# A decay table, modulation rows and one value half at other places in a two-layer backbone kernel

## The chip, the cores and the metric

The kernel runs on one core of a Trainium2 chip, in one launch. The metric is the device time of an execution in microseconds (us), as a median of several runs. TensorE (PE) multiplies matrices, VectorE (DVE) and ScalarE (ACT) work elementwise on tiles of 128 partitions, GpSimd (POOL) and SyncE (SP) here do little but issue transfers. Products land in PSUM, which has eight banks of 128 x 512 float32.

## The reference, cut to what matters

Latent tokens x (512 x 1024) and context tokens (256 x 1024) pass through two layers. Each layer normalises its input and modulates it with a shift, a scale and a gate computed from a conditioning vector:

```python
silu_c = jax.nn.silu(c)
for i in range(DEPTH):                       # DEPTH = 2
    shift_x, scale_x, gate_x = jnp.split(silu_c @ ada_w[i] + ada_b[i], 3, axis=-1)
    hx = rmsnorm(x, norm_g[i]) * (1 + scale_x[:, None]) + shift_x[:, None]
    # layer 0: retention over latent and context tokens; layer 1: chunked gMLP
    x = x + gate_x[:, None] * out_x
return rmsnorm(x, final_g)

def retention_mixer(hx, hc, w_in, decay_logit, w_out, need_ctx):
    log_g = jax.nn.log_sigmoid(decay_logit)
    qc, kc, vc, zc = retention_project(hc, w_in)     # 4 heads: q, k 256 wide, v, z 512 wide
    qx, kx, vx, zx = retention_project(hx, w_in)
    qx, kx = axial_rope(qx, row, col), axial_rope(kx, row, col)
    # scores q k^T times powers of the head's decay, in both directions, then times v
    out_x = retention_output(ox, zx, w_out)          # rmsnorm, times silu(z), times w_out
```

The output is the latent stream. Layer 0's context output is not needed for it.

## The kernel before, in words

**Numbers.** Products take float32 operands cut into a high and a low part (`split`, L132: ACT writes the high part with a CAST, DVE subtracts it to get the low part), and `mm3` (L126) does three matmuls for one. In the profile such a pair is `hl`: the CAST `hl<-raw` on ACT, then `hl<-raw,hl` on DVE.

**Projections of layer 0.** The input projection is worked off in pieces called kq, v and z of a head. Each piece is one 2x2 block product done by the seven products of a Strassen-like scheme, in the order `SINGLE` = B11, T1, T2, B21, T3, B22, T4. Each product is 24 matmuls of 128 x 256 (twelve more for the context tokens of a v piece, 24 for those of B11 and B21 of a kq piece). `Product.run` gives their banks: B11, T2, T3 and T4 share bank x; T1 and B22 share z; B21 has y. After B11, T1 and T2 ACT copies the bank away (`snap<-pst`, called snap); after B21, B22 and T3 DVE adds the bank onto such a copy (`snap<-snap,pst`, called plus). So T4 may write bank x only after the plus of T3 has read it. z and y are taken from a ring of two banks with the tag `tm`, and whatever else asks for a `tm` bank stands in the same ring.

**The loop that is changed (L1142).** It runs over nine pieces; I call them n = 0 to 8: kq1, v1, z1, kq2, v2, z2, z3, kq3, v3, the digit being the head. `i` counts the seven products within one. After a product, the text hangs other work there:

- `step()` is one step of `background` (L987): the modulation rows of the next layer, four pieces. One of the pieces 0 to 2 has twelve steps: one load, eight that multiply a row of weights by one conditioning number and add it up on DVE (`ada_a<-bg,cpad,ada_a`; a load of the next row stands ahead of each of the first seven), an empty one, then two for the columns. The first column step (`columns`, L968) takes a `tm` bank and does four matmuls `pst<-ada_a,ones`, and ACT copies the bank (`cole<-pst`). The second takes another `tm` bank for two transposes `pst<-ident,cole`, and DVE copies out 128 x 8. `row_tags` names the buffers that rows are loaded to, `bg_raw` deals them out in turn.
- `aside(dec0)` is one of three steps of `decay(0)` (L1039): a 512 KB table is loaded, ACT takes two exponentials of 128 x 512 (`bg<-bg,lg`), DVE combines them into `dt`. Head 0's attention needs `dt`.
- `aside(qk0)` and `aside(v0)` load head 0's q, k, v and z back from DRAM and cut them (`halves`, L1063: `v<-v` first on ACT, then on DVE).
- `between_modes` (L361) puts a `pst<-ones` matmul where the operands change from one kind to another.
- `popped` finishes a product of kq: rope on DVE (`rope_a`, `rope_b`) and a transfer to DRAM by POOL.

PE keeps the order of the text. On ACT and DVE a scheduler of the tile layer orders by its own estimates; an instruction written within `aside` may not stand ahead of the one before it in the text (`Queue`, L54, which is why nearly every row of the profile says L54).

After the loop comes `attend` (L1172) for head 0, whose third score product needs the bank that the first `pf<-pst,dt` of DVE has read (two `tm` banks again).

Of the kernel before, what the change touches and what calls it, by code (L numbers as in the profile page):

```python
# [67 lines left out]
def hybrid_kernel(ctx, tc, xT_d, cT_d, cv_d, sv_d, rows_d, ada0_d, adag_d, w_d, rope_d, dec_d, ws_d, id_d, out_d):  # L68
# [464 lines left out]
    g0 = sv[:, 32:48].rearrange("p (k r) -> p k r", r=2)  # L533
# [174 lines left out]
    def project(q):  # L708
        if q[0] == "kq":
            return Product(features, kq_done(q[1]), hc)  # L710
        if q[0] in ("v", "z"):
            return Product(tokens, wide_done(*q), ctx=(CA, vc_d[q[1]]) if q[0] == "v" else None)
        return Product(tokens, vz_done(q[1], q[2]), hc)
# [234 lines left out]
    row_tags = ["g0", "s3"]  # L948
# [76 lines left out]
    def aside(work):  # L1025

        act.pinned = dve.pinned = True
        r = next(work, None)
        act.pinned = dve.pinned = False
        return r  # L1030

    def step():
        return aside(bg)
# [67 lines left out]
    def load_v(h):  # L1101
        v = []
        for tag, src in zip(("oA11", "oS1", "oS2"), (*v_d[h], vc_d[h])):
            v.append(st([P, 2, 2, 512], tag, F32R, name="v"))
            load(f32(v[-1][:, 1]), src)
            yield
        z = st([P, NT, 512], "oA12", name="z")
        for t in range(2):
            load(z[:, 2 * t:2 * t + 2, :], z_d[h][t])
        yield  # L1110
        for x in v:
            halves(x)
            yield
        vv[h] = v, z
        yield

    def popped():
        if later:
            later.pop(0)()

    def drained(gen):
        for _ in gen:
            pass
# [15 lines left out]
    pieces = []  # L1139
    qk0 = load_qk(0)  # L1140
    v0 = load_v(0)
    for n, q in enumerate(QUADS[3:]):  # L1142
        pr = project(q)
        if n in (2, 6):
            row_tags[:] = ("g0", "s3", "g2") if n == 2 else ("s3", "g2")
        if n in (1, 4, 8):
            inside_t.append(between_modes)
        if n in (0, 3, 7):
            inside.append(between_modes)
        for i, name in enumerate(SINGLE):  # L1150
            pr.run(name, Q.get())
            if i in (1, 5) if n == 0 else i % 2:
                popped()
            if (n, i) in ((0, 3), (0, 5), (1, 0), (1, 2)):
                aside(ctx_sum)
            if 2 not in pieces and i in {0: (2, 4, 6), 1: (1, 3, 5, 6), 2: (1, 5), 5: (1, 5), 6: (1, 5)}.get(n, range(7)):
                pieces.append(step())
            if n == 6 and i % 2 == 0:
                aside(dec0)
            if n == 8:  # L1160
                aside(qk0)
                if i > 2:
                    aside(qk0)
            if n == 8:
                aside(v0)
    drained(dec0)
    drained(qk0)
    drained(v0)
# [585 lines left out]
```

## Time and profile before

| what | us |
|---|---|
| median of three runs | 870.85 (870.5 to 871.86) |
| the profiled execution's own time | 869.74 |
| its span in the profile | 868.0 |
| PE busy | 856.9 (99%) |
| DVE busy | 699.5 (81%) |
| ACT busy | 463.6 (53%) |
| POOL busy | 78.4 (9%) |

The span is the time from the first to the last recorded instruction; the execution's own time is 1.74 us longer. The mean granted PE clock is 0.998 of full speed. A row of a timeline reads: start, duration, engine, line, operation, out<-in, shapes, how many in a run, and in brackets the idle time of that engine just before, with what ended it. `snap<-snap,pst` on DVE is a plus, `snap<-pst` on ACT is a snap.

### The profile page before, as it was taken

The numbers are of one execution on the slowest core, as the hardware profiler recorded it, in microseconds if no ns is written. First come the engines' busy times: TensorE is split into PE (matmuls) and PEld (weight loads), VectorE is DVE, ScalarE is ACT, GpSimd is POOL, SyncE is SP. The second block draws the span as 40 slices with busy tenths as digits, with TensorE's granted clock in tenths as the row PEclk, the third lists the DMA queues.
The fourth block names the chain that finished last, engine by engine and source line by source line (L and its number), as shares of the span: only waits on it lengthen the run. The fifth ranks groups of instructions, "written<-read, shape, count | busy, mean of one in ns | idle before, by whom it ended". The sixth has DMA issues, their size and how long they took to land.

```text
span 868.0 us, 17070 instructions
## 1 busy us (share of the span) xinstructions
PE 856.9 (99%) x6870; PEld 819.6 (94%) x6870; DVE 699.5 (81%) x1007; ACT 463.6 (53%) x726; POOL 78.4 (9%) x119
## 2 busy tenths in 40 slices
PE   8999999999999999999999999999999999999997
PEld 7899999999999898999989899999999899899986
DVE  4799899869867985878676669998888478678895
ACT  5466644444368345727363549754667456255434
POOL 0001211211211010000000002021000000000110
PEclk9999999999999999999999999999999999999999
DMA  9945867877867898757164622666556256146522
GB/s 359 405 128 150 252 188 265 259 209 210 282 182 240 270 322 293 256 165 242 64 227 138 213 55 110 211 167 222 168 146 194 49 147 204 39 147 195 120 44 104
DMA packets 77551, 165.88 MB, mean 191 GB/s; under 512 B 8096, under 2 KB 33184, under 8 KB 77472
## 3 DMA queue, kind: packets, MB, share of 16 engines
q1 hardware_dynamic: 65856, 128.40, 44.1%
q0 software_dynamic: 11184, 36.18, 16.2%
q8 instruction: 54, 0.88, 0.4%
q10 hardware_dynamic: 432, 0.20, 0.1%
q14 instruction: 25, 0.20, 0.1%
HBM read 128.58 MB, written 24.12 MB: 176 GB/s over the span
## 4 chain that ended last, share of the span: by engine, by line
PE 74%; issue 12%; DVE 5%; DMA 5%; POOL 2%; ACT 1%; POOLq 0%; DVEq 0%; SPq 0%; ACTq 0%
PE pst L54 74%; DMA ada_w<-in_ada_dram 2%; DVE hl L54 2%; DMA bg<-in_adag_dram 1%; DVE ada_a L54 1%; DMA cq<-in_cT_dram 1%; POOL raw L186 1%; DVE rope_a L54 1%; DMA z<-snap 1%; DVE raw L54 1%; POOL z L142 0%; DMA cv<-in_cv_dram 0%; POOL v L142 0%; DVE o L54 0%; DVE cs L54 0%
## 5 line engine op out<-in xcount | busy, mean ns | idle before, releaser
L54 DVE TENSOR_TENSOR hl<-raw,hl 128x1024 fp32r<-128x1024 f32 (+2 forms) x197 | 235.4, 1199 | 70.5 <-ACT hl L54 70.1
L54 ACT CAST hl<-raw 128x1024 fp32r<-128x1024 f32 (+2 forms) x197 | 202.1, 1031 | 141.9 <-PE pst L54 59.3
L54 PE MATMUL pst<-hl,oS 128*128 128x256 f32 x1152 | 134.6, 276 | 0.0
L54 PEld LDWEIGHTS pst<-hl,oS 128*128 128x128 f32 x1152 | 132.3, 188 | 0.4 <-ACT ctx L54 0.4
L54 PE MATMUL pst<-oS,hl 128*128 128x256 f32 x1104 | 132.3, 277 | 0.0
L54 PEld LDWEIGHTS pst<-oS,hl 128*128 128x128 f32 x1104 | 128.1, 188 | 0.8 <-issue 0.8
L54 PE MATMUL pst<-oA,hl 128*128 128x256 f32 x936 | 117.0, 280 | 1.6 <-DVE snap L54 1.5
L54 PEld LDWEIGHTS pst<-oA,hl 128*128 128x128 f32 x936 | 110.7, 188 | 3.8 <-DVE snap L54 1.7
L54 PE MATMUL pst<-hl,oA 128*128 128x256 f32 x768 | 92.4, 277 | 0.0
L54 PE MATMUL pst<-og,hl 128*128 128x256 f32 x768 | 91.1, 278 | 0.0
L54 PEld LDWEIGHTS pst<-hl,oA 128*128 128x128 f32 x768 | 89.3, 188 | 0.4 <-ACT hl L54 0.4
L54 PEld LDWEIGHTS pst<-og,hl 128*128 128x128 f32 x768 | 89.2, 188 | 0.3
L54 DVE TENSOR_TENSOR raw<-raw 128x1024 f32<-128x1024 f32 x69 | 84.1, 1220 | 0.7
L54 ACT ACTIVATE snap<-pst 128x512 f32<-128x512 f32 x75 | 44.6, 595 | 67.2 <-PE pst L54 67.2
L54 PE MATMUL pst<-v,ph 128*128 128x512 f32 x192 | 59.8, 393 | 0.0
L54 PE MATMUL pst<-hl,ya 128*128 128x512 f32 (+1 forms) x246 | 59.1, 386 | 0.0
L186 POOL DMA_DIRECT2D raw<-raw x23 | 20.5, 891 | 388.3 <-ACT hl_e L54 173.3
L54 PEld LDWEIGHTS pst<-hl,ya 128*128 128x128 f32 x246 | 45.3, 188 | 9.4
L54 DVE TENSOR_TENSOR snap<-snap,pst 128x512 f32<-128x512 f32 x69 | 47.0, 681 | 5.8 <-PE pst L54 5.7
L54 ACT CAST ph<-pf 128x512 fp32r<-128x512 f32 x24 | 14.8, 618 | 57.3 <-DVE pf L54 57.3
L54 PEld LDWEIGHTS pst<-v,ph 128*128 128x128 f32 x192 | 36.1, 188 | 7.0
L54 DVE SCALAR_TENSOR_TENSOR acc<-pst,gate,acc 128x256 f32<-128x256 f32 x64 | 29.3, 479 | 12.8 <-PE pst L54 12.7
(207 smaller groups left out, 1105.2 us busy)
## 6 DMA issues: line engine op xcount, KB each, us to landing
raw<-in_w_dram SPq DMA_DIRECT2D x224, 256.0 KB, 3.9
bg<-in_adag_dram SPq DMA_DIRECT2D x32, 512.0 KB, 5.0
raw<-raw POOLq DMA_DIRECT2D x23, 512.0 KB, 4.7
ada_w<-in_ada_dram SPq DMA_DIRECT2D x16, 512.0 KB, 8.7
raw<-in_w_dram SPq DMA_DIRECT2D x16, 512.0 KB, 4.5
bg<-in_dec_dram SPq DMA_DIRECT2D x12, 512.0 KB, 5.4
v<-snap POOLq DMA_DIRECT2D x16, 256.0 KB, 4.1
z<-snap POOLq DMA_DIRECT2D x16, 256.0 KB, 3.9
```

The lines of the kernel that those rows point to most:

```text
L54: made = op(*args, **kw)
L186: nc.gpsimd.dma_start(self.raws[q, "12"], self.raws[q, "22"], accum_op=ALU.add)
```

## The change

Three things in the loop over n, and no arithmetic is changed:

- the three steps of head 0's decay table stand after products 1, 3 and 5 of n = 3 (q and k of head 2) where they stood after products 0, 2 and 4 of n = 6 (z of head 3);
- the steps of the modulation rows are dealt out anew: one more at n = 2, four for seven at n = 3, and three for two at n = 5 and n = 6. By the end of n = 6 both kernels have done 27, so n = 7 and 8 are as before. The buffers for rows go with it: `g0` is left out from n = 2 to n = 3 while the decay table uses it, and again from n = 7;
- after product 5 of n = 8 (v of head 3) a second step of `load_v(0)` follows the first.

```diff
     for n, q in enumerate(QUADS[3:]):
         pr = project(q)
-        if n in (2, 6):
-            row_tags[:] = ("g0", "s3", "g2") if n == 2 else ("s3", "g2")
+        if n in (2, 4, 7):
+            row_tags[:] = ("g0", "s3", "g2") if n == 4 else ("s3", "g2")
...
-            if 2 not in pieces and i in {0: (2, 4, 6), 1: (1, 3, 5, 6), 2: (1, 5), 5: (1, 5), 6: (1, 5)}.get(n, range(7)):
+            if 2 not in pieces and i in {0: (2, 4, 6), 1: (1, 3, 5, 6), 2: (1, 3, 5), 3: (0, 2, 4, 6), 5: (1, 3, 5), 6: (1, 3, 5)}.get(n, range(7)):
                 pieces.append(step())
-            if n == 6 and i % 2 == 0:
+            if n == 3 and i % 2:
                 aside(dec0)
...
             if n == 8:
                 aside(v0)
+                if i == 5:
+                    aside(v0)
```

How instructions move is shown at three places.

ACT in z of head 3 (n = 6), a piece of the difference (`bg<-bg,lg` are the exponentials, `snap<-snap` the silu of a finished block, `ACT_TABLE_LOAD` stands where ACT changes from one function to the other):

```order
-L54 ACTIVATE snap<-pst 128x512
-L54 ACT_TABLE_LOAD
-L54 ACTIVATE bg<-bg,lg 128x512 x2
-L54 ACTIVATE snap<-pst 128x512
-L54 CAST hl<-raw 128x1024 x2
-L54 ACTIVATE snap<-pst 128x512
-L54 ACTIVATE bg<-bg,lg 128x512 x2
-L54 CAST hl<-raw 128x1024 x2
-L54 ACT_TABLE_LOAD
-L54 ACTIVATE snap<-snap 128x512 x2
-L54 ACT_TABLE_LOAD
-L54 ACTIVATE bg<-bg,lg 128x512 x2
```

The six exponentials and all four changes of function leave this piece. Two changes are left in all: one ahead of the exponentials in kq of head 2, one ahead of the first silu in z of head 2.

PE in z of head 2 (n = 5), before, from the first product's `hl_2989` on (`oA11` is B11, `oS1` T1, `oS2` T2, `oA12` B21, `oS3` T3):

```order
L54 MATMUL pst_3086<-ada_a_2623,ones_126 32x256 x4
L54 MATMUL pst_3096<-hl_2989,oA11_328 128x256 x24
L54 MATMUL pst_3126<-hl_3041,oS1_861 128x256 x24
L54 MATMUL pst_3153<-ident_130,cole_3091 128x128 x2
L54 MATMUL pst_3156<-ones_126 128x128
L54 MATMUL pst_3096<-hl_3093,oS2_1012 128x256 x24
L54 MATMUL pst_3200<-hl_3123,oA12_570 128x256 x24
L54 MATMUL pst_3096<-hl_3161,oS3_1239 128x256 x24
```

and now:

```order
L54 MATMUL pst_3107<-hl_3003,oA11_328 128x256 x24
L54 MATMUL pst_3137<-hl_3058,oS1_861 128x256 x24
L54 MATMUL pst_3107<-hl_3104,oS2_1012 128x256 x24
L54 MATMUL pst_3203<-hl_3134,oA12_570 128x256 x24
L54 MATMUL pst_3231<-ada_a_2672,ones_126 32x256 x4
L54 MATMUL pst_3107<-hl_3164,oS3_1239 128x256 x24
L54 MATMUL pst_3137<-hl_3196,oS4_1173 128x256 x24
L54 MATMUL pst_3305<-ident_130,cole_3236 128x128 x2
```

The column step of the second row piece has moved from ahead of B11 to behind B21. Its `pst_3231` has the bank of `pst_3203`, since the other bank of the `tm` ring holds `pst_3137`, which B22 still adds to; it waits for the plus that reads `pst_3203`.

DVE at the end of v of head 3 (n = 8), before:

```order
L54 TENSOR_TENSOR v<-v 128x1024
L54 TENSOR_TENSOR snap<-snap,pst 128x512
L54 TENSOR_TENSOR ctx<-ctx,pst 128x256
L54 TENSOR_TENSOR v<-v 128x1024
L54 SCALAR_TENSOR_TENSOR pf<-pst,dt 128x512
```

and what the difference says there:

```order
 L54 TENSOR_TENSOR v<-v 128x1024
 L54 TENSOR_TENSOR snap<-snap,pst 128x512
+L54 TENSOR_TENSOR v<-v 128x1024
 L54 TENSOR_TENSOR ctx<-ctx,pst 128x256
 L54 TENSOR_TENSOR qk<-qk 128x512 x2
```

The last `v<-v` (the low part of head 0's context v) stands one product earlier, behind the plus of T3, and no longer right ahead of the first `pf`. Its CAST on ACT moves in the same way, ahead of T4's snap.

## The prediction, made before the result was known

> **What bounds the kernel now.** The profile's first part names the engine: PE is busy 856.9 of 868.0 us. So I looked for the holes in PE, first in its waits by what ended them (behind the start-up, one for a DVE `snap` and one for a DVE `pf`), then with windows between the two. Columns of a window: length, then busy time of PE, PEld, DVE, ACT, POOL (with counts), the granted clock, the DMA share, GB/s.
>
> ```profile
> 105.00:293.00 188.00, 187.97 (x1657) 186.70 (x1656) 162.83 (x201) 93.44 (x126) 31.52 (x47) 1.00 0.74 233
> 296.00:331.00 35.00, 35.00 (x310) 34.46 (x310) 27.13 (x41) 14.55 (x22) 5.46 (x9) 1.00 0.88 280
> ```
>
> From 105 to 331 us PE stands still in two places only, near 294 and near 331. The clock is 1.00 throughout. What the change can win lies in these two holes; what it can lose are new ones. A full PE does 48 matmuls in 200.72 - 195.28 = 5.44 us (first two rows below), 0.1133 each and 2.72 per product of 24.
>
> *The hole near 294* is in kq of head 3, between B22 and T4:
>
> ```profile
> 195.28 5.60 PE L54 MATMUL pst<-oS,hl 128*128 128x256 f32 x48
> 200.72 2.88 PE L54 MATMUL pst<-oA,hl 128*128 128x256 f32 x24
> ...
> 285.52 2.88 PE L54 MATMUL pst<-hc,hl 128*128 128x256 f32 x24
> 288.24 5.60 PE L54 MATMUL pst<-oS,hl 128*128 128x256 f32 x48
> 288.30 0.68 DVE L54 TENSOR_TENSOR snap<-snap,pst 128x512 f32<-128x512 f32 x1
> 294.61 0.68 DVE L54 TENSOR_TENSOR snap<-snap,pst 128x512 f32<-128x512 f32 x1
> 295.35 1.87 PE L54 MATMUL pst<-oA,hl 128*128 128x256 f32 x14 [1.50 <-DVE snap L54]
> 298.19 0.88 PE L54 MATMUL pst<-hl,oA 128*128 128x256 f32 x6
> ```
>
> T4 could start at 288.24 + 5.44 = 293.68; it starts at 295.35, and the next product at 298.19 instead of 296.40. The hole costs 1.79 us. T4 waits for the plus of T3 (294.61 + 0.68 = 295.29, and 0.06 more). DVE is late as a whole: it does B21's plus at 288.30, though PE left B21's latent part at 285.52, 0.20 before DVE could read (192.56 and 192.76 in kq of head 2, below). From plus to plus it is busy without a break, 295.29 - 288.30 = 6.99 us. Why it is late stands one piece earlier, in z of head 3:
>
> ```profile
> 256.08 1.28 ACT L54 ACT_TABLE_LOAD   x1
> 257.38 1.34 ACT L54 ACTIVATE bg<-bg,lg 128x512 f32<-128x512 f32 x2
> 261.47 1.33 ACT L54 ACTIVATE bg<-bg,lg 128x512 f32<-128x512 f32 x2
> 264.75 1.28 ACT L54 ACT_TABLE_LOAD   x1
> 269.45 1.28 ACT L54 ACT_TABLE_LOAD   x1 [1.45 <-DMA bg<-in_dec_dram]
> 270.75 1.34 ACT L54 ACTIVATE bg<-bg,lg 128x512 f32<-128x512 f32 x2
> 272.11 1.28 ACT L54 ACT_TABLE_LOAD   x1
> 273.94 1.03 ACT L54 CAST hl<-raw 128x1024 fp32r<-128x1024 f32 x1
> 272.12 0.69 DVE L54 TENSOR_TENSOR dt<-bg 128x512 f32<-128x512 f32 x1 [1.17 <-ACT bg L54]
> 275.00 1.23 DVE L54 TENSOR_TENSOR hl<-raw,hl 128x1024 fp32r<-128x1024 f32 x1 [2.19 <-ACT hl L54]
> ```
>
> ACT waits for the last table, changes its function and comes to kq3's first CAST at 273.94 only; DVE stands still for 1.17 and 2.19 us and never makes it up (19.53 us busy of the 20 from 276, in the windows below).
>
> *The hole near 331* is the third score product of head 0:
>
> ```profile
> 324.00 0.68 DVE L54 TENSOR_TENSOR snap<-snap,pst 128x512 f32<-128x512 f32 x1
> 328.31 2.99 PE L54 MATMUL pst<-qk 128*128 128x256 f32 x24
> 328.77 1.05 ACT L54 CAST v<-v 128x1024 fp32r<-128x1024 f32 x1
> 329.86 1.23 DVE L54 TENSOR_TENSOR v<-v 128x1024 fp32r<-128x1024 f32 x1 [4.84 <-ACT v L54]
> 331.00 0.68 DVE L54 SCALAR_TENSOR_TENSOR pf<-pst,dt 128x512 f32<-128x512 f32 x1
> 331.74 1.68 PE L54 MATMUL pst<-qk 128*128 128x256 f32 x12 [0.44 <-DVE pf L54]
> ```
>
> It could start at 328.31 + 2.72 = 331.03 and starts 0.71 later, because `pf` stands behind a `v<-v` whose CAST came last on ACT. With a slow second matmul, as in the other hole, I count 0.75.
>
> **The change part by part.** *Decay table out of z3.* ACT loses 1.34 + 1.33 + 1.34 + 4 x 1.28 = 9.13 us there, and DVE the `dt` work (0.69 for each full part, 0.76 for the divided one in a row below). B21's plus in kq3 must come 288.30 - 285.72 = 2.58 earlier to be on time; the last `dt` and the two standstills alone are 0.69 + 1.17 + 2.19 = 4.05. Then DVE's 6.99 end at 292.7 against 293.68: the hole goes, with 1.0 to spare. Steps at n = 7 are the same as before, so nothing is added in that stretch. -1.79; bounds -1.79 and, should half of the lateness stay, -0.9.
>
> *Decay table into kq2.* The windows say where DVE has room:
>
> ```profile
> 182.00:201.00 19.00, 18.96 (x169) 18.24 (x168) 11.51 (x16) 6.98 (x9) 2.27 (x3) 1.00 0.47 152
> 220.00:240.00 20.00, 20.00 (x180) 19.46 (x179) 17.03 (x24) 8.08 (x11) 5.86 (x9) 1.00 0.81 259
> 276.00:296.00 20.00, 18.50 (x163) 18.30 (x162) 19.53 (x21) 8.68 (x11) 2.44 (x4) 1.00 0.72 247
> ...
> 192.56 2.88 PE L54 MATMUL pst<-hc,hl 128*128 128x256 f32 x24
> 192.76 0.69 DVE L54 TENSOR_TENSOR snap<-snap,pst 128x512 f32<-128x512 f32 x1 [0.68 <-PE pst L54]
> 194.82 0.76 DVE L54 TENSOR_TENSOR rope_a<-rope_a,rope_b 128x256 f32<-128x256 f32 x2
> 198.97 0.68 DVE L54 TENSOR_TENSOR snap<-snap,pst 128x512 f32<-128x512 f32 x1
> 262.84 0.76 DVE L54 TENSOR_TENSOR dt<-bg 128x384 f32<-128x384 f32 x2 [0.30 <-ACT bg L54]
> ```
>
> In kq2 (182 to 201) DVE is idle for 7.5 us and ACT for 12. The first `dt` fits ahead of B21's plus. Between it and T3's plus stand now, in addition, one low half of `hl` (1.14 from row to row, as from 329.86 to 331.00; formerly ahead of B21's plus) and `dt` of 0.76. Laid end to end from 192.76: plus 0.60, low half 1.14, rope 2.1 (its last row ended at 195.58, 2.2 behind the plus), `dt` 0.7, low half 1.14, sum of two weights 1.14, plus 0.68, which ends near 200.3. T4 is due at 200.72: 0.4 to spare instead of 1.07 (198.97 + 0.68 = 199.65). If DVE absorbs nothing of the 1.90 added, the plus ends at 201.55 and T4 is 0.89 late. I take 0.10, since a missing 0.4 would need a late CAST.
>
> The Trainium skill ("ScalarE: Activation LUTs", What ACT_TABLE_LOAD costs) gives a change of function 1.28 us for the load and 1.38 more for a drain. The load is 1.28 in these rows too, but the next function starts 1.30 after the load's start both times (257.38, 270.75), so no drain shows. By the page the casts behind kq2's new change would be 1.38 later, and its T4 some 0.6 late: an estimate that ends at the second rival below.
>
> *Steps of the modulation rows.* The second piece's column step now follows B21 in z2 and needs the bank of B21. PE must wait until DVE has read it: 0.20 from PE's last result to DVE (192.56 to 192.76), 0.68 for the plus, 0.06 back to PE (295.29 to 295.35), together 0.94. Before, the same four matmuls stood ahead of B11 with no wait:
>
> ```profile
> 232.36 0.64 PE L54 MATMUL pst<-ada_a,ones 128*32 128x256 f32 x8
> 232.93 3.00 PE L54 MATMUL pst<-hl,oA 128*128 128x256 f32 x24
> 242.36 1.04 ACT L54 CAST hl<-raw 128x1024 fp32r<-128x1024 f32 x1
> 243.43 1.23 DVE L54 TENSOR_TENSOR hl<-raw,hl 128x1024 fp32r<-128x1024 f32 x1 [1.95 <-ACT hl L54]
> ```
>
> Nothing in the sequence lets PE go past it, so the whole round trip is lost. DVE is just free to take it. Without the matmuls of the column steps ahead of it PE comes to B21 at 232.36 + 3 x 2.72 = 240.52, 1.15 sooner than before; T4's CAST and low half (242.36 and 243.43 before) depend on ACT's copy of T2's bank and come sooner with it, at 241.21 and 242.28, and DVE is free at 243.44. PE leaves B21 at 243.24, readable at 243.44. I take 0.90, as the switch to another operand costs 0.12 in any place (232.36 to 232.93 is 0.57 for four matmuls). Bounds: 0 if the bank is read in time, 2.08 if that low half is first in the queue. Its followers lie later in z2 with 2 us to spare, so the delay is paid once.
>
> Two of the second piece's rows of `ada_a` (about 1.2 each from row to row) go on DVE from kq2 to the end of v2, where 2.97 us are idle (220 to 240). They stand ahead of T2's low half in z2, and so does now the low half of B21:
>
> ```profile
> 202.09 1.27 DVE L54 SCALAR_TENSOR_TENSOR ada_a<-bg,cpad,ada_a 128x1024 f32<-128x1024 f32 x1
> 232.81 2.45 DVE L54 TENSOR_TENSOR hl<-raw,hl 128x1024 fp32r<-128x1024 f32 x2 [1.17 <-ACT hl L54]
> ```
>
> T2's low half was done at 234.04 and comes to 234.04 + 1.14 + 2.4 - 1.17 = 236.4, with T2 due at 232.36 + 5.44 = 237.80; without the 1.17 of idle time as cover it comes at 237.57, still in time. So nothing. On SP the tables and rows are issued at other places of its queue, each where a buffer is free; no load of weights stands behind a new wait there.
>
> *v half one product sooner.* The last low half stands one product sooner, and what follows it on DVE moves by at most 1.14: B22's plus (324.00) then ends at 325.8, and PE next needs its bank at 328.31. Its load is issued where it was; should it land late, DVE waits for it ahead of T4's score banks, which is the bound of no gain. `pf` can start at 328.31 + 1.36 + 0.20 = 329.87, ends at 330.55, and the third score starts on time. -0.75; bounds -0.75 and 0.
>
> **Sum.** -1.79 - 0.75 + 0.90 + 0.10 = -1.54. The profiled execution's own time of 869.74 (span 868.0 and 1.74 around it) goes to 868.2; the median stands 1.11 above that execution, so **869.3**.
>
> **The rivals.** *No wait at the column step* (12%): DVE's plus is done before PE gets there, or PE finds another bank. For it: the column step of before shows no wait (232.36). Against it: that one found both banks free, and behind B21 nothing stands in between. Then -1.79 - 0.75 + 0.10 = -2.44, 868.4.
>
> *The hole moves to kq2* (20%): the added 1.90 us is not absorbed and T4 waits 0.89 there, or a part of the hole in kq3 stays: -1.54 - 0.10 + 0.89 = -0.75, 870.1. For it: only 0.4 us of room by my layout. Against it: DVE's 7.5 us of idle time in kq2. The drain of the Trainium skill leads here too.
>
> *DVE is full in both kq pieces* (8%, slower): kq3's hole isn't ACT's doing but DVE's, with 19.53 of 20 us busy; then it stays, and kq2, given the table, gets one of its own. It decides if B21's plus in kq3 still comes after 285.72 + 1.0 = 286.7. Then 0 - 0.75 + 0.90 + 0.89 = +1.04, 871.9. Against it: the standstills of 1.17 and 2.19 just ahead.
>
> *The moves change nothing that PE waits for* (4%): the holes stay, the column step finds its bank: 870.85.
>
> **How the numbers follow.** The forecast has 56%, with its own range 868.8 to 870.0 (0.5 for the column step and for kq2). A difference below 0.2%, 1.74 us, can't be told from none here; the border is at 869.11. The forecast lies just inside: a third of its chance falls beyond, 0.20; with the first rival and a few hundredths of the second I say faster 0.35, slower 0.08 (the rival that says so), and the rest, 0.57, no change. The range that holds 8 in 10 goes from 868.0, below the first rival, to 870.9, beyond the second.
>
> **What would show it.** Right: no wait for `snap` in kq3, with ACT's `hl` CASTs ahead of it near 269; no wait for `pf` near 331; a new wait of PE on DVE `snap` in z2, ahead of four `pst<-ada_a,ones`, with about 0.7 idle; B21's plus in kq3 0.2 after PE. Wrong: a hole ahead of T4 in kq2 over 0.3; a hole in kq3 left; a column step longer than 1.5; holes at some place that I haven't named, such as T2 of z2 waiting for `hl`.

## The result, and the profile after

The changed kernel takes 869.97 us (median of 20 runs, 868.54 to 871.71), the kernel before 871.85 in 20 runs beside it (870.5 to 873.23). The ratio is 0.9979, with a 95% interval from 0.9973 to 0.9986: 1.8 us less, between 1.2 and 2.4. The forecast was 1.5 less.

The profiled execution of the changed kernel took 870.49 us with a span of 868.7, which is longer than the profiled 869.74 and 868.0 of before. The profiled execution of before was faster than any of its 20 timed runs (the lowest is 870.50), that of the changed kernel slower than its median. So the spans alone would mislead; what counts is where PE stands still. The waits of PE after (us in total, times, longest):

```profile
PE pst L54 <- DMA ident<-in_id_dram: 1.9, 1, 1.9
PE pst L54 <- DVE eps L54: 1.1, 1, 1.1
PE pst L54 <- DVE snap L54: 0.8, 1, 0.8
PE pst L54 <- DVE pf L54: 0.2, 1, 0.2
```

The first two belong to the start-up. The one wait for a `snap` is a new one, in z of head 2; the one for `pf` is another than before, in head 1's scores. Laid out as in the prediction, windows after:

```profile
105.00:241.00 136.00, 135.97 (x1198) 135.24 (x1197) 122.48 (x159) 65.16 (x91) 22.78 (x35) 1.00 0.78 242
241.00:246.00 5.00, 4.22 (x40) 3.61 (x39) 3.12 (x4) 3.24 (x4) 0.00 (x0) 1.00 0.81 259
246.00:331.00 85.00, 85.00 (x751) 84.46 (x750) 67.52 (x83) 39.46 (x55) 14.80 (x22) 1.00 0.78 243
```

From 105 to 331 us there is one hole where there were two, at 244 to 245, and PE is full from 246 to 331.

A ledger over the whole span can be made from the trace, since both kernels start the same number of recorded matmuls (6870) in nearly the same order: the time from the start of matmul number a to that of number b, before and after.

```
stretch (matmul numbers)             before    after   difference
0 to 298     start-up                 34.53    35.48     +0.95
298 to 2030  up to v2                196.23   196.21     -0.02   (T4 of kq2 lies here)
2030 to 2145 z2 up to T3              12.91    13.75     +0.84   column step
2145 to 2560 up to B22 of kq3         47.14    47.15     +0.01
2560 to 2600 around T4 of kq3          6.32     4.53     -1.79
2600 to 2880 up to head 0's scores    31.76    31.72     -0.04
2880 to 2910 head 0's scores           5.17     4.44     -0.73
2910 to 3240 head 0's attention       44.83    45.01     +0.18
3240 to 3310 head 1's scores          11.43    12.06     +0.63
3310 to 4450                         152.46   152.53     +0.07
4450 to 4640 layer 1                  21.64    22.30     +0.66
4640 to the last matmul              296.26   296.26      0.00
```

The stretch from the start-up's end to matmul 2910, in which all the terms of the forecast lie, is 1.73 us shorter. Start-up (PE waits 1.9 for `ident<-in_id_dram` there, before 1.2) and three later entries, of 0.18, 0.63 and 0.66, add what makes this one execution longer; the later ones are taken up below.

The places themselves, in the timeline after. Kq of head 3:

```profile
269.25 1.05 ACT L54 CAST hl<-raw 128x1024 fp32r<-128x1024 f32 x1 [2.23 <-DVE raw L54]
287.29 2.88 PE L54 MATMUL pst<-hc,hl 128*128 128x256 f32 x24
287.49 0.69 DVE L54 TENSOR_TENSOR snap<-snap,pst 128x512 f32<-128x512 f32 x1
290.01 5.60 PE L54 MATMUL pst<-oS,hl 128*128 128x256 f32 x48
293.81 0.68 DVE L54 TENSOR_TENSOR snap<-snap,pst 128x512 f32<-128x512 f32 x1
295.45 2.88 PE L54 MATMUL pst<-oA,hl 128*128 128x256 f32 x24
```

ACT comes to kq3's first CAST at 269.25, where it came to it at 273.94 before, and now after a wait of 2.23 for DVE's `raw`. B21's plus begins at the first possible moment, 0.20 behind PE (before: 2.78 behind). T3's plus ends at 294.49, 0.96 ahead of T4, which follows B22 without a break (290.01 + 5.44 = 295.45).

Z of head 2, the column step:

```profile
241.35 2.88 PE L54 MATMUL pst<-hl,oA 128*128 128x256 f32 x24
243.12 1.23 DVE L54 TENSOR_TENSOR hl<-raw,hl 128x1024 fp32r<-128x1024 f32 x1 [1.49 <-ACT hl L54]
244.28 0.69 DVE L54 TENSOR_TENSOR snap<-snap,pst 128x512 f32<-128x512 f32 x1
245.02 0.64 PE L54 MATMUL pst<-ada_a,ones 128*32 128x256 f32 x8 [0.78 <-DVE snap L54]
```

B21 is through at 241.35 + 2.72 = 244.07. The plus starts at 244.28, 0.21 behind it and in the moment in which DVE has laid down a low half, and the four small matmuls start at 245.02, 0.95 late.

Kq of head 2 on ACT, DVE and PE, and head 0's first scores:

```profile
188.09 1.28 ACT L54 ACT_TABLE_LOAD   x1
189.38 1.33 ACT L54 ACTIVATE bg<-bg,lg 128x512 f32<-128x512 f32 x2
200.55 0.68 DVE L54 TENSOR_TENSOR snap<-snap,pst 128x512 f32<-128x512 f32 x1
201.65 2.88 PE L54 MATMUL pst<-oA,hl 128*128 128x256 f32 x24
...
324.71 0.68 DVE L54 TENSOR_TENSOR snap<-snap,pst 128x512 f32<-128x512 f32 x1
328.25 4.40 PE L54 MATMUL pst<-qk 128*128 128x256 f32 x36
329.86 0.69 DVE L54 SCALAR_TENSOR_TENSOR pf<-pst,dt 128x512 f32<-128x512 f32 x1 [4.13 <-PE pst L54]
```

T3's plus in kq2 ends at 201.23, 0.42 ahead of T4. The three score products run on as 36 matmuls; `pf` now waits for PE and not for a `v<-v`.

### The profile page after: what moved, and what is told of

The parts are those of the page before. It is cut to its first block, busy times and chain, and to the rows that moved or that the text cites. A ratio compares the mean times of both kernels' runs of the same rounds, so it can differ in the third digit from the quotient of the medians.

```text
span 868.7 us, 17062 instructions
## 1 busy us (share of the span) xinstructions
PE 858.7 (99%) x6870; PEld 822.4 (95%) x6870; DVE 698.8 (80%) x1007; ACT 461.4 (53%) x724; POOL 78.1 (9%) x119
## 4 chain that ended last, share of the span: by engine, by line
PE 94%; DMA 2%; DVE 1%; ACT 1%; issue 1%; ACTq 0%; DVEq 0%
PE pst L54 94%; DMA bg<-in_dec_dram 1%; DMA ident<-in_id_dram 1%; ACT junk L54 0%; DMA bg<-in_adag_dram 0%; DVE o L54 0%; ACT bg L54 0%; DVE acc L54 0%; DVE v L54 0%; DVE ada_a L54 0%; ACT L54 0%; DVE hl L54 0%; ACT hl L54 0%; ACT fss L54 0%; DVE dt L54 0%
```

## The experiments

Two questions stood open. Did the hole in kq3 go because ACT was freed in z3, or because the new wait in z2 gave DVE 0.8 us? And is the new wait the bank's, so that it can be had for nothing? A third came with the ledger: whether head 1 takes a part back. All ratios are against the kernel before, run on the same chip beside the others.

**The column step one product later.** The changed kernel with

```diff
-5: (1, 3, 5), 6: (1, 3, 5)}
+5: (1, 4, 5), 6: (1, 3, 5)}
```

> The changed kernel with one step moved: the column step of the second row piece stands behind T3 of z2 in place of behind B21. My theory: its bank was read one product earlier, so the new wait of about 0.8 us in z2 goes, and nothing else changes: no hole ahead of T4 in kq3, none near 331. That is about 2.6 us less than before, a ratio near 0.9970 (the changed kernel's is 0.9979). Rival 'the wait pays for the hole': kq3's hole is closed only because the wait in z2 gave DVE 0.8 us; then a hole of about 0.8 comes back ahead of T4 in kq3, and the ratio stays near 0.9979. Rival 'given back in head 1': PE comes earlier to the attention of head 1 and waits there for a table that comes by its own clock, so the ratio stays near 0.9979 with a hole near 380 that is 0.8 longer.

868.93 us, ratio 0.9964 (0.9952 to 0.9976). Z of head 2 in its timeline:

```profile
241.14 2.88 PE L54 MATMUL pst<-hl,oA 128*128 128x256 f32 x24
243.86 2.88 PE L54 MATMUL pst<-hl,oS 128*128 128x256 f32 x24
246.67 0.64 PE L54 MATMUL pst<-ada_a,ones 128*32 128x256 f32 x8
247.24 3.00 PE L54 MATMUL pst<-hl,oS 128*128 128x256 f32 x24
```

The column step comes 0.09 behind T3, and the stretch 2030 to 2145 is 13.03 against 13.75. The stretch around T4 of kq3 is 4.53, exactly as in the changed kernel: no hole. So the wait did not pay for it, and the first rival falls. The last one doesn't hold either: head 1's stretch (3240 to 3310) is 11.63, shorter than the changed kernel's 12.06.

**The v half alone.** The kernel before with

```diff
                 aside(v0)
+                if i == 5:
+                    aside(v0)
```

> The kernel before with only the last half of head 0's v one product sooner. My theory: the hole near 331 goes, 0.7 us, ratio 0.9992; the hole ahead of T4 in kq3 stays at 1.8. Rival 'given back in head 1': the hole near 331 goes and one of 0.5 to 0.7 appears near 380, ratio 0.9998 or more.

870.44 us, ratio 0.9986 (0.9977 to 0.9995), 1.2 us less with an interval from 0.4 to 2.0 (one of its eleven runs took 4942 us and is left out of the ratio). The score stretch is 4.44 as in the changed kernel, the kq3 hole is there (6.26), head 1's stretch is 11.76, 0.33 longer than before. Its profiled execution has a hole of its own, which no other shows:

```profile
315.55 0.62 ACT L54 CAST qk<-qk 128x512 fp32r<-128x512 f32 x1 [3.97 <-DMA qk<-q]
316.51 1.65 PE L54 MATMUL pst<-hl,hc 128*128 128x256 f32 x12 [1.48 <-ACT ctx L54]
```

A late `qk` transfer kept ACT for 3.97 us, and a copy of `ctx` queued behind it held up PE. The three other kernels with the earlier v half don't have this hole; it shows how far one profiled execution can stray here.

**The table alone.** The kernel before with the table in kq2 and the buffers for rows that go with it, the steps as before:

```diff
-        if n in (2, 6):
-            row_tags[:] = ("g0", "s3", "g2") if n == 2 else ("s3", "g2")
+        if n in (2, 4, 7):
+            row_tags[:] = ("g0", "s3", "g2") if n == 4 else ("s3", "g2")
...
-            if n == 6 and i % 2 == 0:
+            if n == 3 and i % 2:
```

> The kernel before with only the decay table moved to kq2 (and the buffers for rows as in the changed kernel), the steps as before. My theory: the hole in kq3 goes, since ACT in z3 is free of exponentials, and the one near 331 stays at 0.7; no wait in z2. With seven steps of rows in kq2 beside the table, T4 of kq2 may wait up to 0.9 there. 1.8 less to 0.9 less, ratio 0.9979 to 0.9990. Rival 'the wait pays for the hole': without the wait in z2 a hole of about 0.8 is left in kq3, ratio 0.9988. The profile tells the two apart by the place.

872.9 us, ratio 1.0012 (1.0002 to 1.0022): slower. Kq3's hole is gone (4.53) without any wait in z2; since PE was held up in v2 here, this run alone would not refute the rival. But neither my theory nor the rival had the price: the stretch up to v2's end (1826 to 2030) is 26.18 against 23.12, in a place that neither had named.

```profile
207.95 1.28 DVE L54 SCALAR_TENSOR_TENSOR ada_a<-bg,cpad,ada_a 128x1024 f32<-128x1024 f32 x1 [3.44 <-DMA bg<-in_adag_dram]
220.64 2.88 PE L54 MATMUL pst<-hl,oS 128*128 128x256 f32 x24
225.49 0.42 DVE L54 TENSOR_TENSOR ctx<-pst,ctx 128x256 f32<-128x256 f32 x1
225.96 1.68 PE L54 MATMUL pst<-hl,cs 128*128 128x256 f32 x12 [2.44 <-DVE ctx L54]
```

With seven steps of rows in kq2 as well, DVE stands at a row's transfer for 3.44 us early in v2, and then is full of rows, rope and low halves; its `ctx` comes at 225.49, and PE waits 2.44 for it. Kq2's T4 does not wait. From there to B22 of kq3 this one execution is 1.47 longer still, without a wait, in matmuls of a slower pace (the last section).

**The steps alone.** The kernel before with the changed table of steps, the decay table still in z3:

```diff
-i in {0: (2, 4, 6), 1: (1, 3, 5, 6), 2: (1, 5), 5: (1, 5), 6: (1, 5)}
+i in {0: (2, 4, 6), 1: (1, 3, 5, 6), 2: (1, 3, 5), 3: (0, 2, 4, 6), 5: (1, 3, 5), 6: (1, 3, 5)}
```

> The kernel before with only the steps of the rows dealt out anew, the decay table still in z3. My theory: the wait of 0.8 at the column step in z2 is there, and kq3's hole is still there: as long as before if ACT's lateness moves with PE (0.8 slower, ratio 1.0010), 0.8 shorter if it hangs on a transfer's own clock (no change). The one near 331 stays. Rival 'the wait pays for the hole': kq3's hole is gone though the table is still in z3, about 1.0 less, ratio 0.9989.

871.81 us, ratio 1.0000 (0.9992 to 1.0009). The waits of PE for `snap` in z2 and in kq3:

```profile
244.99 0.64 PE L54 MATMUL pst<-ada_a,ones 128*32 128x256 f32 x8 [0.78 <-DVE snap L54]
290.52 5.60 PE L54 MATMUL pst<-oS,hl 128*128 128x256 f32 x48
297.44 2.78 PE L54 MATMUL pst<-oA,hl 128*128 128x256 f32 x22 [1.32 <-DVE snap L54]
```

Both are there: the column's, and kq3's, where T4 starts 1.48 late (290.52 + 5.44 = 295.96) for 1.67 before. By the stretches that is +0.84 and -0.18 (6.14 for 6.32), and 0.54 more in between, where PE waits for a low half of DVE at 282.23. As long as the table is in z3, the hole stays, though PE came 0.84 + 0.54 = 1.4 later to it. In the trace that adds up to 1.2 more, while the medians are the same within 0.8; the stretches are taken against one execution of before, and a fast one.

**Without the exponentials.** The kernel before with a scaled copy in place of `Exp` for head 0:

```diff
-AF.Exp, scale=lg[:, h:h + 1])
+AF.Exp if h else AF.Identity, scale=lg[:, h:h + 1])
```

(and the same in the second half).

> The kernel before with the exponentials of head 0's table left out: ACT passes the loaded numbers through a scaled copy that needs no change of function, so three of the four changes of function in z3 go (head 0's attention then computes with a wrong table). Transfers, the same six passes of 128x512 on ACT and the dt work on DVE stay in z3. My theory, ACT was late from the changes of function and the wait for the table: without 3 x 1.28 us the first CAST of kq3 comes 2.5 to 3.8 earlier, DVE's plus of B21 in kq3 is at most 0.5 late, and the hole ahead of T4 goes: 1.8 less, ratio 0.9979. Rival 'DVE is too full': the dt work and the low halves stay, so the hole stays above 0.9, ratio 0.9990 or more. Rival 'the transfer': ACT waits for the third table by the transfer's own clock; only the last change of function is saved, about 1.3 of the 2.58 us, and a hole near 0.5 is left, ratio 0.9985.

869.14 us, ratio 0.9982 (0.9972 to 0.9992). In its timeline:

```profile
270.48 1.34 ACT L54 ACTIVATE bg<-bg,lg 128x512 f32<-128x512 f32 x2 [1.61 <-DMA bg<-in_dec_dram]
271.72 1.04 ACT L54 CAST hl<-raw 128x1024 fp32r<-128x1024 f32 x1
286.46 2.88 PE L54 MATMUL pst<-hc,hl 128*128 128x256 f32 x24
287.76 0.68 DVE L54 TENSOR_TENSOR snap<-snap,pst 128x512 f32<-128x512 f32 x1
289.18 5.60 PE L54 MATMUL pst<-oS,hl 128*128 128x256 f32 x48
294.80 3.01 PE L54 MATMUL pst<-oA,hl 128*128 128x256 f32 x24
```

All four changes of function are gone from z3, where I had expected three. T4 starts 0.18 late (289.18 + 5.44 = 294.62); the stretch is 4.84, so 1.48 of the 1.79 went with the changes of function. My theory had most of it, but not the whole: B21's plus is still 1.10 late (287.76 for 286.66) where I had said 0.5 at most. ACT still waits 1.61 for the third table and comes to the CAST at 271.72, against 269.25 in the changed kernel, which is what the rival 'the transfer' says. The other 0.31 is left to the transfers, the six passes on ACT and the `dt` work, which stay in z3 here; this run doesn't tell them apart.

**Another bank for the column step.** The changed kernel, its PE and DVE order untouched:

```diff
-    def columns(a, dst):
-        pr = pt((P, HS), tag="tm")
+    def columns(a, dst, tag="tm"):
+        pr = pt((P, HS), tag=tag)
...
-                yield from columns(a, sh1)
+                yield from columns(a, sh1, "ps")
```

> The changed kernel, every instruction in its order on PE and DVE, but the second row piece's column step takes its bank from the ring of six that the x banks use. My theory, the wait in z2 is for B21's bank alone: it goes though the step still stands behind B21, 0.8 less than the changed kernel, the same time as with the step moved behind T3 (ratio 0.9964 to 0.9970). Rival 'the place': four small matmuls of another kind right behind B21 cost their 0.8 anyway (ratio 0.9979). Should the stretch of slower matmuls in the next layer (547 to 564 us, 0.118 us each for 0.1133) be the changed kernel's own, it shows here as well.

868.65 us, ratio 0.9969 (0.9957 to 0.9980).

```profile
241.40 2.88 PE L54 MATMUL pst<-hl,oA 128*128 128x256 f32 x24
244.21 0.64 PE L54 MATMUL pst<-ada_a,ones 128*32 128x256 f32 x8
244.78 5.73 PE L54 MATMUL pst<-hl,oS 128*128 128x256 f32 x48
```

Same place, other bank, no wait: the column step starts 0.09 behind B21, and the stretch is 12.91, as before the change. The wait was the bank's, 0.84 us by the ledger. The Trainium skill ("PSUM — Partial Sum Buffer", Summary: rules for kernel authors) says to aim at a different bank while one is being read. This run shows that rule with its price in this kernel.

**Without the v half.** The kernel of the last experiment without the second `aside(v0)`:

> The kernel with the other bank for the column step, and the last half of head 0's v where it was before the change: table and steps without the third part. The kernels with the earlier v half show a hole of 0.2 to 0.6 us near 380 in head 1's attention, and 0.18 of slower matmuls near 330; those without show neither. Theory 'partly given back': the hole near 331 is back (0.73), the one near 380 and the slower matmuls are gone, so this kernel is no more than 0.5 slower than the one with all three (ratio near 0.9975 against 0.9969), and faster than the changed kernel as measured only by the bank. Rival 'fully worth it': the hole near 380 is there here too (PE comes early from table and steps), and the ratio is 0.9978 or more. Rival 'nothing left of it': ratio 0.9969 or less.

869.26 us, ratio 0.9968 (0.9956 to 0.9980).

```profile
326.68 2.99 PE L54 MATMUL pst<-qk 128*128 128x256 f32 x24
330.11 1.65 PE L54 MATMUL pst<-qk 128*128 128x256 f32 x12 [0.44 <-DVE pf L54]
...
376.06 2.88 PE L54 MATMUL pst<-qk 128*128 128x256 f32 x24
379.22 1.65 PE L54 MATMUL pst<-qk 128*128 128x256 f32 x12 [0.28 <-DVE pf L54]
```

Head 0's hole is back (5.17, starting 0.71 late), and head 1's is there too (12.01, 0.44 late), without the v half. So the hole near 380 isn't the v half's, against 'partly given back'. One part of that theory stands: head 0's attention (2910 to 3240) takes 44.83 here, as in the four other kernels without the earlier v half (44.83 to 44.84), and 45.01 in each of the four with it; by the traces 0.18 of the 0.73 is given back there. By its place the hole near 380 speaks for 'fully worth it', by its ratio this run falls to 'nothing left of it', and the times of this kernel and of the one with the v half can't be told apart (0.9968 and 0.9969, each plus or minus 0.0012). So what the v half is worth in time is known only from the run that has it alone, 0.4 to 2.0 us.

Three kernels without the column wait, the one with the step moved, the one with the other bank, and the last, stand at 0.9964 to 0.9969: all beat the kernel before, by 2.7 to 3.1 us. By their ratios they are also about 1 us faster than the changed kernel, but their intervals overlap with one another and with its 0.9973 to 0.9986, so that the 0.84 of the bank is shown in the traces and not by the times.

## Why the prediction was right, and where it wasn't

**The time.** -1.54 was forecast, -1.83 measured (1.22 to 2.35). The median of 869.97 lies above the forecast 869.3 although the gain was larger, since the kernel before has a median of 871.85 in 20 runs and had 870.85 in the three that were shown. That the ledger's -1.73 comes so near to -1.83 is in part luck: the two profiled executions as wholes differ by +0.75, and the sum leaves out the start-up and everything behind matmul 2910, of which one execution can't say how much is the change's.

**Term by term**, from the ledger:

| step | forecast | in the trace |
|---|---|---|
| decay table out of z3, hole in kq3 | -1.79 | -1.79 |
| B21's plus in kq3 behind PE | 0.20 | 0.20 |
| room ahead of kq3's T4 | 1.0 | 0.96 |
| T4 of kq2: room, and cost | 0.4, +0.10 | 0.42, 0 |
| column step in z2 | +0.90 | +0.84 |
| v half, head 0's scores | -0.75 | -0.73 |
| T2 of z2 | 0 | 0 |
| sum | -1.54 | -1.68, and -1.73 for the stretch |

**What carried.** The order rows named the wait, and the rows of before priced it: nothing in the trace of before shows a matmul that waits for a bank of the `tm` ring behind B21, but its three parts were there (0.20, 0.68, 0.06), and the sum came within 0.06. That PE comes to B21 about 1.15 sooner (1.27, with the later start-up taken off), so that DVE is just free, was right as well: DVE was through with its low half at 244.28 and began the plus in that moment.

**What the steps were for: wrong.** The prediction took the new spread of the modulation rows as a cost (0.90) with nothing on the other side, and kept a hole in kq2's T4 as the place where the table could hurt. The run with the table alone shows the other side: with the old spread the table costs 3.06 us up to v2's end, one piece later than I had looked. The forecast was right about the changed kernel, since there the layout of kq2 and z2 was made from the order after; it would have been wrong about the parts. The rival 'the hole moves to kq2' had the idea that the work isn't absorbed, but in the wrong place: a hole near T4 of kq2 shows in none of the runs.

**DVE or ACT.** 'DVE is full in both kq pieces' is refuted by the changed kernel (plus 0.20 behind PE) and from the other side by the run without exponentials, where 1.48 of 1.79 go while all of DVE's work stays.

**The drain.** The second rival leaned also on a page of the Trainium skill ("ScalarE: Activation LUTs", What ACT_TABLE_LOAD costs), by which 1.38 us of drain come on top of the load. In kq2 the load takes the page's 1.28, but the exponentials start 1.29 behind the load's start (188.09, 189.38). No drain shows, and T4 kept its 0.42. For the 0.6 that the prediction gave as T4's delay by that page it shows no working; 1.38 less the room of 0.4 would be 0.98.

**What was not foreseen.** Head 1's scores are 0.63 longer in the profile of the changed kernel, where a `pf` of DVE comes late and the third score product starts at 380.17 instead of 377.07 + 2.72 = 379.79:

```profile
375.47 1.28 DVE L54 SCALAR_TENSOR_TENSOR ada_a<-bg,cpad,ada_a 128x1024 f32<-128x1024 f32 x1 [1.75 <-DMA bg<-in_adag_dram]
377.07 2.88 PE L54 MATMUL pst<-qk 128*128 128x256 f32 x24
379.44 0.68 DVE L54 SCALAR_TENSOR_TENSOR pf<-pst,dt 128x512 f32<-128x512 f32 x1
380.17 1.65 PE L54 MATMUL pst<-qk 128*128 128x256 f32 x12 [0.22 <-DVE pf L54]
```

The stretch is 0.20, 0.33, 0.61 and 0.58 longer in four of the experiments (step moved, v half alone, other bank, no v half) and not at all in the three others. It doesn't follow the v half, as the last run shows. The traces say what is late: in eight of the nine, that of before among them, DVE's last standstill ahead of this `pf` is for a modulation row, as at 375.47, and the `pf` starts 3.96 to 3.97 behind its end, since DVE has work without a break in between. The stretch is longer in just those five in which PE begins the scores 1.50 to 1.91 behind the end of that standstill; in the others of the eight it is 2.16 to 2.39 (before: 2.16). What sets the row's time against PE's, and whether most executions have this hole, was not settled.

## What to carry to other kernels

Where PE is full, look at the two or three places where it isn't, and ask for each who was late one stage earlier; here the cause lay some 20 us ahead of the wait, for the most part in another engine's changes of function. Here a small product that asked for a bank in the middle of a sequence cost a whole round trip to the engine that empties the bank (0.84 us): a ring of two was too short for a guest, and a bank from another ring took the wait away. Work that moves into a stage takes room from what is already there: the table's move alone made the kernel about 1 us slower (0.2 to 1.9) although it closed the hole in kq3, and only with the rows spread anew was the 1.79 there a gain of the whole.

## What the runs showed of the hardware

Matmuls of the same shape run at two paces at the full granted clock. Windows over the same stretch of layer 1, before the change and after (the numbers in brackets behind PE's busy time are its matmuls):

```profile
548.00:562.00 14.00, 14.00 (x126) 14.00 (x125) 14.00 (x16) 10.78 (x14) 1.09 (x2) 1.00 0.67 216
```

```profile
548.00:562.00 14.00, 14.00 (x121) 14.00 (x120) 14.00 (x16) 10.94 (x14) 1.09 (x2) 1.00 0.68 217
```

121 matmuls where 126 were, 0.118 us from start to start instead of 0.1133 (the counts take in those that an edge of the window cuts), with the clock at 1.00 in both rows and no wait recorded. That is the +0.66 of the ledger. It shows in the changed kernel, in the one with the step moved and in the last one, and not in the one with the other bank (126 in that window), whose PE and DVE order is that of the changed kernel. The run with the table alone has such a pace at another place, between 227 and 279 us of its trace. What sets the pace was not found.
